# Projecting the values of two kinds of heads with tokens on partitions, ahead of the attention

## The chip, the cores and the metric

The kernel runs on one core of a Trainium2 chip. The metric is the device time of one execution in microseconds; the time of a version is the median of its runs. The core has five engines that work side by side, each through its own instructions in order: TensorE (PE, matmuls; its loads of the stationary operand are listed as PEld), VectorE (DVE), ScalarE (ACT), GpSimd (POOL) and SyncE (SP), from whose queue all transfers of this kernel are issued. Matmuls write to PSUM, from which ACT or DVE evict. Everything else lives in SBUF (128 partitions) or in DRAM.

## What is computed

One layer of a hybrid decoder on 1024 tokens of width 1024, in float32: half a SwiGLU, then a mixer of two groups of heads, then another half SwiGLU and a gated embedding. The change touches only the mixer:

```python
u = rmsnorm(h, mix_norm[i])
z = u @ w_in[i]
m_qk, m_v, m_o, m_if, f_q, f_k, f_v, f_f = jnp.split(z, split_idx, axis=-1)
m_qk = jax.nn.silu(causal_depthwise_conv(m_qk, conv_qk[i]))
...
h_m = mlstm_chunkwise(...)          # 4 heads, values m_v of width 128
...
h_f = forgetting_attention(...)     # 8 heads, values f_v of width 64
...
h = h + jnp.concatenate([y_m, y_f], axis=-1) @ w_out[i]
```

Both m_v and f_v are 512 columns of z. In the FoX attention a value block of 128 keys by 64 columns is multiplied from the right to the probabilities of 128 queries; in the mLSTM a block of 128 tokens by 128 columns goes into the state and into the output of a chunk. Both need the values with tokens on partitions.

## The kernel before

**Precision.** Matmuls run in float32r. Each operand is split into hi (a rounded copy, made by ACT) and lo (the rest, a subtraction on DVE, or on POOL where `aside` is set); `split_from` (line 100) does this. `mm3` (line 93) adds the three products hi·hi, hi·lo and lo·hi, so a product over k = 1024 for 512 columns takes 8 k tiles x 3 = 24 matmuls.

**The input of the mixer** is `xt`: the normalized tokens, transposed, so that a k tile has 128 channels on partitions and 512 tokens in its row, as (hi, lo), for each half of the tokens and each half of k.

**Projections.** `proj_stream` (line 625) takes jobs of 128 columns of w_in. Weights of a job are loaded in one transfer (`raw_cols`, line 57), split one job ahead, and used as the stationary operand; xt is the moving one. The result of a job and a half of the tokens is one PSUM bank with 128 columns of z on partitions and 512 tokens in a row. A sink takes it from there. For values a sink copies it to SBUF with ACT, PE transposes its four blocks of 128 x 128, and an eviction puts them where the attention reads them: for the mLSTM `v_sink` and `v_turn` (lines 867 to 879) into `v1`; for FoX `v_sink` and its `back` (lines 1073 to 1088) into `V[p]`, one tile for a pair of heads, which holds hi and lo side by side.

**Order of the mixer.** `mlstm` (line 831) first weaves the gates (DVE and ACT work, lines 716 to 828, with their tiles in the pool `gp`) with the projections of q and k, whose sink adds the convolution (DVE) and the Silu (ACT). Then the mLSTM values are projected, lines 894 to 899. Then the chunks run (`main`, line 901), with the output gate's projection as fill. `fox` (line 1026) projects values, queries and keys of the first pair of heads (line 1236) and then weaves `attention()` with `fill()`: the projections of the other three pairs, in the order values, queries, keys, and then `out_m`, the mLSTM part of the output projection (line 1259).

**weave** (line 605) emits two streams so that they advance together: each yields its time on PE as an estimate, and fill is emitted until it has `frac` times what the main stream has. A stream that can't go on yields None. In `jobs(p)` (line 1091) values of pair p may start when the values of the head that last used their buffer are done (`used`), queries and keys when the scores of the head that last used their tiles are done (`free`). A head is scores (line 1098: two or three matmuls for each 128 queries and 512 keys, a maximum on DVE, an exponential on ACT), transposes of the probabilities (line 1161), their split, and products with `V` (line 1141). Some work is put off by a number of steps with `later` (line 1174). `attention()` waits at the head of each pair until `done["proj"]` says that its keys are there.

The program's order is not kept to the letter: the compiler orders instructions of an engine by priority (their order in the program) among those that it takes to be ready, and it places tiles in pools, where a tile waits until the one that had its place before is done with.

Of the kernel before, what the change touches and what calls it, by code (L numbers as in the profile page):

```python
# [16 lines left out]
P = 128  # L17
# [7 lines left out]
# pairs of dff tiles, and the order of the seven block products of a Winograd form  # L25
# [4 lines left out]
class Net:  # L30
# [26 lines left out]
    def raw_cols(self, w, c0):  # L57
        """128 columns of a [1024, N] weight: row k * 128 + p at [p, k]."""
        r = self.rp.tile([P, KT, P], F32, tag="raw", name="raw")
        self.nc.sync.dma_start(out=r, in_=w[:, c0:c0 + P].rearrange("(k p) n -> p k n", p=P))  # L60
        return r
# [6 lines left out]
    def split(self, raw, pool=None, tag="w", aside=False):  # L68
        """raw = hi + lo, both in float32r."""
# [7 lines left out]
    def split2(self, raw, aside=False):  # L77
        """The two halves of k of a weight tile, each (hi, lo)."""
        return [self.split(raw[:, 4 * j:4 * j + 4, :], aside=aside) for j in range(2)]
# [13 lines left out]
    def mm3(self, out, ahi, alo, bhi, blo, first, last):  # L93
        """out (+)= a.T @ b with a = ahi + alo and b = bhi + blo."""
# [5 lines left out]
    def split_from(self, hi, lo, src, aside=False):  # L100
        """src (PSUM or SBUF) = hi + lo; aside: on GpSimd (SBUF only)."""
# [8 lines left out]
    def norm_rows(self, src, gain, dst):  # L110
        """dst = RMSNorm(src) * gain for 128 tokens; dst also takes the squares."""
# [7 lines left out]
    def xunit(self):  # L119
        """Four k tiles by 512 columns, (hi, lo)."""  # L120
        return tuple(self.xp.tile([P, 4, 512], F32R, tag=t, name=t) for t in ("xhi", "xlo"))

    def new_xt(self):
        """[half of the tokens][half of the k tiles] -> (hi, lo)"""
        return [[self.xunit() for _ in range(2)] for _ in range(2)]

    def normer(self, src, gain, dst):
        """RMSNorm of one token tile after another, transposed and split into dst(i) -> (hi, lo).
        Returns step(i), which takes token tile i and finishes the one before; step.rows(i) only takes it,
        step.next() only finishes the oldest."""  # L130
# [31 lines left out]
    def wino_put(self, B, name, rows, i):  # L162
        """512 columns of token tile i, transposed, into a right operand."""
# [10 lines left out]
    def wino_normer(self, src, gain, B, rows, bufs):  # L174
        """RMSNorm of one token tile after another into the right operands of the seven products
        (x transposed: rows k < 512 and k >= 512, columns t < 512 and t >= 512, Winograd's form).
        Three operands wait in DRAM for wino_rest. step(i) takes token tile i and finishes the one
        before, step.last() finishes the last."""
# [43 lines left out]
    def wino_rest(self, B, name):  # L222
        """One of the operands that wait in DRAM, through its place for lo."""
# [9 lines left out]
    def swiglu(self, B, w_gate, w_up, pools):  # L233
        """hidD = silu(x @ w_gate) * (x @ w_up), transposed, by pairs of dff tiles; the products of a
        pair (2 x 2 blocks: dff tile, half of k, half of the tokens) in Winograd's form with seven
        block products, each of three float32r products."""
# [3 lines left out]
        def pair(m, which, s):  # L240
            """Appends the seven products of the dff tiles m, m + 1."""
# [13 lines left out]
            # the first pair's tile a is loaded again for the sums  # L255
# [18 lines left out]
            def slot(r, c):  # L274
                """Where block (dff tile r, token half c) is put together."""
# [7 lines left out]
            def out(r, c, x, y, t):  # L283
                """Block (r, c) is x + y."""
# [8 lines left out]
            def hidden(r, c):  # L293
                """The left operands of the product with w_down: A11 = H00, A12 = H10, A21 = H01, A22 = H11
                (H: dff tile, half of the tokens), S1 = A21 + A22, S2 = S1 - A11, S3 = A11 - A21, S4 = A12 - S2."""
# [58 lines left out]
            # block (0, 0) = P1 + P2, (0, 1) = P1 + P6 + (P5 + P3), (1, 1) = P1 + P6 + P7 + P5,  # L354
            # (1, 0) = P1 + P6 + P7 + P4 (T4 is negated)
# [3 lines left out]
        for m in range(0, DFF // P, 2):  # L359
            s = {}  # L360
            g, u = pair(m, 0, s), pair(m, 1, s)
            # the first products don't need the second half of the tokens, those after them not T2, T3, T4
# [20 lines left out]
    def down(self, h, w_down, hook):  # L383
        """h += 0.5 * hid @ w_down in Winograd's form (2 x 2 blocks: half of the tokens, parity of the dff
        tile, half of the columns), one of the seven products after the other. Yields after the first loads
        and after the first operands; hook(j, q) runs after pair q of product j (the last one in two parts,
        4 and 8, of 256 tokens each)."""
# [20 lines left out]
        def fetch(j, q):  # L408
            """The left operands of two pairs."""
# [11 lines left out]
        def prep(n):  # L421
# [19 lines left out]
            # in place: T1 = B12 - B11, T3 = B22 - B12, T2 = B22 - T1, T4 = B21 - T2  # L441
# [18 lines left out]
        with tc.tile_pool(reuse_waits="tile", name="dn", bufs=1, side="right") as dn, \  # L460
# [11 lines left out]
            def evict(j, i):  # L472
                """Returns what can wait."""
# [18 lines left out]
            # C11 = P1 + P2, C12 = P1 + P6 + P5 + P3, C22 = P1 + P6 + P7 + P5, C21 = P1 + P6 + P7 + P4  # L492
            # (T4 is negated)
# [22 lines left out]
    def ffn(self, h, gain, w_gate, w_up, w_down, norms, hook, bufs, early=False, release=None):  # L516
        """h += 0.5 * SwiGLU(RMSNorm(h)); norms(step, prepare, products, pools, load_gain) runs the normalization
        over the token tiles, prepare() has the first weights split; early: products(n) may run there."""
# [39 lines left out]
    def ple_rows(self, p, w_proj, ps):  # L558
        """ppD = p @ w_proj; yields after every product of 128 tokens by 512 columns."""
# [45 lines left out]
def weave(main, fill, frac):  # L605
    """Emit main and fill so that they advance together: fill gets frac of main's TensorE time.
# [904 lines left out]
```

## Time and profile before

| | |
|---|---|
| runs shown, median (lowest to highest) | 2029.75 us (2027.75 to 2033.62), 3 runs |
| span of the profiled execution | 2033.1 us |
| mLSTM values, projections of lines 896 to 899 | from 756.4 to about 806 us |
| chunks of the mLSTM | 806 to 896 us |
| first FoX projections | 896 to 927 us |
| FoX attention with its fill | 931 to 1215 us |
| rest of out_m, then the output projection | from 1215 us |

The page gives no time of the profiled execution other than its span; the span lies between the median and the highest of the runs shown. In the views, a row of a timeline has start, duration, engine, line, operation, operands and, in brackets, the idle time of the engine before it with what ended it. A row of a table of stretches has the stretch and its length, then for each engine the busy time with the number of instructions, then the granted TensorE clock, the DMA engines' busy share and GB/s. A row of a group ends with busy time, mean ns of one, and the idle time before its instructions. Matmuls are pipelined: a row's duration overlaps that of its neighbours, so the distance of starts, not the duration, is what a matmul takes of PE.

### The profile page before, as it was taken

How to read it: one execution, taken by the hardware profiler on the slowest of the kernel's cores; microseconds unless marked ns; L12 is line 12 of the kernel's file. 1: busy time of each engine (PE TensorE's matmuls, PEld its weight loads, DVE VectorE, ACT ScalarE, POOL GpSimd, SP SyncE). 2: the span in 40 equal slices, each digit the busy share in tenths (PEclk: the TensorE clock that was granted, in tenths of full speed). 3: DMA queues.
4: the chain of work that ended last, by engine and by line, in shares of the span. 5: the costliest groups of instructions: out<-in, count | busy, mean ns of one | idle time of the engine just before them, and what ended most of it. 6: DMA issues, size and time to landing. Idle time of an engine off the chain costs nothing. (4 is left out here: it accounts for less than half of the span.)

```text
span 2033.1 us, 25588 instructions
## 1 busy us (share of the span) xinstructions
PE 1982.7 (98%) x9251; PEld 1618.8 (80%) x9251; DVE 1408.4 (69%) x2425; ACT 856.9 (42%) x1634; POOL 135.9 (7%) x148
## 2 busy tenths in 40 slices
PE   7999999999999999999999999999999999999998
PEld 6788888888888787788788777788888888888786
DVE  6966766777877683655565665877777777886766
ACT  6433333334445443435565642433333333444443
POOL 2000000000000110121110411100000000000011
PEclk9999999999999999999999999999999999999999
DMA  7623322338432331122112538533223237633422
GB/s 284 207 89 104 112 96 95 104 112 310 149 101 99 111 86 53 42 95 53 53 54 78 190 122 289 197 106 112 94 94 124 89 99 243 234 104 102 131 70 86
DMA packets 205359, 252.62 MB, mean 124 GB/s; under 512 B 12632, under 2 KB 138096, under 8 KB 204464
## 3 DMA queue, kind: packets, MB, share of 16 engines
q1 hardware_dynamic: 205232, 250.99, 37.8%
q8 instruction: 72, 1.18, 0.2%
q14 instruction: 55, 0.45, 0.1%
HBM read 172.18 MB, written 74.58 MB: 121 GB/s over the span
## 5 line engine op out<-in xcount | busy, mean ns | idle before, releaser
L96 PE MATMUL pp<-xhi,whi 128*128 128x512 f32 x704 | 275.6, 391 | 0.5 <-DVE s L272 0.5
L98 PE MATMUL pp<-xhi,wlo 128*128 128x512 f32 x704 | 274.1, 389 | 0.8 <-DVE wlo L103 0.8
L97 PE MATMUL pp<-xlo,whi 128*128 128x512 f32 x704 | 274.7, 390 | 0.0
L102 ACT CAST whi<-raw 128x512 fp32r<-128x512 f32 x180 | 111.3, 621 | 257.4 <-PE pp L97 177.2
L102 ACT CAST whi<-S 128x512 fp32r<-128x512 f32 x176 | 109.5, 622 | 240.8 <-PE pp L97 186.2
L96 PE MATMUL dn<-xhi,whi 128*128 128x512 f32 x528 | 205.7, 390 | 0.1
L97 PE MATMUL dn<-xlo,whi 128*128 128x512 f32 x528 | 205.5, 389 | 0.0
L98 PE MATMUL dn<-xhi,wlo 128*128 128x512 f32 x528 | 205.1, 389 | 0.0
L102 ACT CAST whi<-ar 128x512 fp32r<-128x512 f32 x132 | 82.3, 623 | 183.3 <-PE dn L97 174.8
L98 PEld LDWEIGHTS pp<-xhi,wlo 128*128 128x128 f32 x704 | 132.3, 188 | 29.2 <-DVE wlo L103 1.2
L96 PEld LDWEIGHTS pp<-xhi,whi 128*128 128x128 f32 x704 | 132.3, 188 | 29.1 <-DVE s L272 0.8
L97 PEld LDWEIGHTS pp<-xlo,whi 128*128 128x128 f32 x704 | 132.3, 188 | 27.7 <-DVE xlo L103 0.3
L103 DVE TENSOR_TENSOR wlo<-raw,whi 128x512 fp32r<-128x512 f32 x162 | 110.5, 686 | 59.7 <-ACT whi L102 46.7
L103 DVE TENSOR_TENSOR wlo<-S,whi 128x512 fp32r<-128x512 f32 x176 | 120.1, 682 | 25.8 <-ACT whi L102 25.7
L103 DVE TENSOR_TENSOR wlo<-ar,whi 128x512 fp32r<-128x512 f32 x132 | 90.7, 687 | 63.9 <-ACT whi L102 63.8
L96 PEld LDWEIGHTS dn<-xhi,whi 128*128 128x128 f32 x528 | 99.1, 188 | 21.0 <-DVE t L272 0.5
L98 PEld LDWEIGHTS dn<-xhi,wlo 128*128 128x128 f32 x528 | 99.1, 188 | 20.7
L97 PEld LDWEIGHTS dn<-xlo,whi 128*128 128x128 f32 x528 | 99.1, 188 | 20.6
L272 DVE TENSOR_TENSOR p<-pp,p 128x512 f32<-128x512 f32 x88 | 60.6, 689 | 74.9 <-PE pp L98 74.9
L107 POOL TENSOR_TENSOR r<-v,mhalf 128x1 f32<-128x1 f32 (+1 forms) x56 | 43.9, 784 | 909.6 <-DVE v L116 756.1
L96 PE MATMUL pj<-xhi,whi 128*128 128x512 f32 x248 | 102.6, 414 | 0.1
L97 PE MATMUL pj<-xlo,whi 128*128 128x512 f32 x248 | 97.5, 393 | 0.0
(350 smaller groups left out, 4515.0 us busy)
## 6 DMA issues: line engine op xcount, KB each, us to landing
ar<-hidD SPq DMA_DIRECT2D x60, 512.0 KB, 3.6
hidD<-t SPq DMA_DIRECT2D x110, 256.0 KB, 3.4
raw<-in_ffn_w_gate_dram SPq DMA_DIRECT2D x46, 512.0 KB, 3.9
raw<-in_ffn_w_up_dram SPq DMA_DIRECT2D x46, 512.0 KB, 3.7
raw<-in_w_in_dram SPq DMA_DIRECT2D x24, 512.0 KB, 3.9
hidD<-x SPq DMA_DIRECT2D x44, 256.0 KB, 3.1
ar<-hidD SPq DMA_DIRECT2D x32, 256.0 KB, 2.9
w<-in_ffn_w_down_dram SPq DMA_DIRECT2D x8, 1024.0 KB, 11.1
```

Source lines behind the costliest of these rows:

```text
L96: mm(out, ahi, bhi, start=first, stop=False)
L97: mm(out, ahi, blo, start=False, stop=False)
L98: mm(out, alo, bhi, start=False, stop=last)
L102: self.nc.scalar.copy(out=hi, in_=src)
L103: (self.nc.gpsimd if aside else self.nc.vector).tensor_tensor(out=lo, in0=src, in1=hi.bitcast(F32), op=ALU.subtract)
L107: self.nc.gpsimd.tensor_tensor(out=r, in0=v, in1=self.mhalf[:, :v.shape[-1]], op=ALU.pow)
L272: add = lambda d, x, y: nc.vector.tensor_tensor(out=d, in0=x, in1=y, op=ALU.add)
```

## The change

The values of both groups are projected in `mlstm`, one group after the other, before the chunks. The tokens are now the stationary operand (128 tokens of a k tile of xt), and 512 columns of weights, all of a group, the moving one. A result is one PSUM bank with 128 tokens on partitions and all 512 value columns in its row, so nothing is transposed.

Weights come as four loads of two k tiles with whole rows of 512 columns. Their split tiles have two pools: `va` for k tiles 0 to 3, filled while the last q and k projection runs, and `vb` for k tiles 4 to 7, in the space of the gates' pool once that is closed. The weights of the FoX values replace those of the mLSTM values k tile by k tile during the last token tile. The tiles `G1` and `qw` move into a pool `ml` in the space of `va` and `vb`.

The mLSTM values are evicted by one copy for each token tile. The FoX values are evicted as hi (ACT) and lo (DVE) in the layout of `V` and stored to a new DRAM tile `vD`, 512 KB for each token tile. In `fox`, `load_v(p)` brings back the 1 MB of a pair: pairs 0 and 1 after the first projections, pairs 2 and 3 when the values of the pair before last in the same buffer are done. `jobs(p)` has queries and keys alone, and the `frac` of the weave goes from 1.13 to 0.9. The rest of the diff takes out comments and docstrings.

```diff
+        self.vD = self.dp.tile([P, NT, 4, 4, 64], F32, tag="vD", name="vD")
...
-            G1 = mk.tile([P, 4, S], F32, tag="G1", name="G1")
-            qw = mk.tile([P, 2, S], F32, tag="qw", name="qw")
...
+                        if ct == 3:
+                            weights(C_MV, 0, 4)
...
-            def v_sink(hd):
-                def sink(half, acc):
-                    vt = mt.tile([P, 512], F32, tag="vt", name="vt")
-                    nc.scalar.copy(out=vt, in_=acc)
-                    turned.append((vt, half, hd))
-                return sink
-
-            def v_turn():
-                vt, half, hd = turned.pop(0)
-                pt = N.tr()
-                for j in range(4):
-                    nc.tensor.transpose(pt[:, j, :], vt[:, j * P:(j + 1) * P], N.ident)
-                nc.vector.tensor_copy(out=v1[:, 4 * half:4 * half + 4, hd, 0:128], in_=pt)
...
+            W, raws = {}, {}
+
+            def weights(c0, lo, hi):
+                for k in range(lo, hi):
+                    if k % 2 == 0:
+                        raws[0] = N.rp.tile([P, 2, 512], F32, tag="raw", name="raw")
+                        nc.sync.dma_start(out=raws[0], in_=self.w[k * P:(k + 2) * P, c0:c0 + 512].rearrange("(k p) n -> p k n", p=P))
+                    W[k] = [vp[k // 4].tile([P, 512], F32R, tag=f"{t}{k}", name=t) for t in ("vhi", "vlo")]
+                    N.split_from(W[k][0], W[k][1], raws[0][:, k % 2, :])
+
+            def token_values(c0, after, sink):
+
+                for i in range(NT):
+                    acc = bank()
+                    ts = slice((i % 4) * P, (i % 4) * P + P)
+                    for k in range(KT):
+                        xh, xl = xt[i // 4][k // 4]
+                        N.mm3(acc, xh[:, k % 4, ts], xl[:, k % 4, ts], W[k][0], W[k][1], k == 0, k == KT - 1)
+                        if i == NT - 1:
+                            after(k)
+                    sink(i, acc)
+
+            def mv_sink(i, acc):
+                nc.scalar.copy(out=v1[:, i, :, 0:128], in_=acc.rearrange("p (a b) -> p a b", a=4))
+
+            def fv_sink(i, acc):
+                t = N.rp.tile([P, 4, 4, 64], F32R, tag="raw", name="fv")
+                av = acc.rearrange("p (q a c) -> p q a c", q=4, a=2)
+                nc.scalar.copy(out=t[:, :, 0:4:3, :], in_=av)
+                nc.vector.tensor_tensor(out=t[:, :, 1:3, :], in0=av, in1=t[:, :, 0:4:3, :].bitcast(F32), op=ALU.subtract)
+                nc.sync.dma_start(out=N.vD[:, i], in_=t.bitcast(F32))
+
+            with ExitStack() as vs:
+                vpool = lambda name: vs.enter_context(self.tc.tile_pool(reuse_waits="tile", name=name, bufs=1))
+                vp = [vpool("va")]
+                with self.tc.tile_pool(reuse_waits="tile", name="gp", bufs=1) as gp:
+                    g = self.gates(xt, keep, gp, bank)
+                    next(g)
+                    weave(g, proj_stream(N, self.w, xt, [(C_MQK + ct * P, qk_sink(ct), None) for ct in range(4)], bank, self.begun[1]), 1.7)
+                vp.append(vpool("vb"))
+                weights(C_MV, 4, KT)
+                token_values(C_MV, lambda k: weights(C_FV, k, k + 1), mv_sink)
+                token_values(C_FV, lambda k: None, fv_sink)
+            ml = pool("ml", bufs=1)
+            G1 = ml.tile([P, 4, S], F32, tag="G1", name="G1")
+            qw = ml.tile([P, 2, S], F32, tag="qw", name="qw")
...
-            for n, _ in enumerate(proj_stream(N, self.w, xt, [(C_MV + hd * P, v_sink(hd), None) for hd in range(4)], bank)):
-                if n % KT == 3 and turned:
-                    v_turn()
-            v_turn()
...
-            def v_sink(p):
...
+            def load_v(p):
+                V[p] = xq.tile([P, NT, 4, 64], F32R, tag="V", name="V")
+                nc.sync.dma_start(out=V[p].bitcast(F32), in_=N.vD[:, :, p])
...
-                used = lambda: 2 * p - 2 <= done["values"]
-                return [(C_FV + p * P, v_sink(p), used), (C_FQ + p * P, q_sink(p), free), (C_FK + p * P, k_sink(p), free)]
+                return [(C_FQ + p * P, q_sink(p), free), (C_FK + p * P, k_sink(p), free)]
...
                         if qb == 3:
-                            done["values"] = hd + 1
+                            if hd % 2 and hd < 5:
+                                load_v((hd + 3) // 2)
...
             run_all(proj_stream(N, self.w, xt, jobs(0), bank))
+            for p in range(2):
+                load_v(p)
...
-            weave(attention(), fill(), 1.13)
+            weave(attention(), fill(), 0.9)
```

## What was predicted

> **What bounds the kernel now.** I read the page first (totals, then the 40 slices), then the busy time by stage, then the stage that the change touches instruction by instruction.
>
> ```profile
> span 2033.1 us, 25588 instructions
> PE 1982.7 (98%) x9251; PEld 1618.8 (80%) x9251; DVE 1408.4 (69%) x2425; ACT 856.9 (42%) x1634; POOL 135.9 (7%) x148
> ```
>
> TensorE has work for 98% of the span. The table of stretches (length, then busy us of PE, PEld, DVE, ACT, POOL, then granted clock and DMA share) shows where that holds:
>
> ```profile
> 756.00:770.00 14.00, 14.00 (x65) 11.60 (x64) 11.18 (x15) 6.14 (x5) 0.00 (x0) 1.00 0.20 47
> 770.00:782.00 12.00, 10.92 (x52) 8.75 (x52) 3.94 (x6) 4.29 (x8) 0.00 (x0) 1.00 0.17 45
> 782.00:806.00 24.00, 24.00 (x113) 19.30 (x112) 5.39 (x9) 5.09 (x9) 0.00 (x0) 1.00 0.16 44
> 896.00:927.00 31.00, 31.00 (x142) 25.66 (x141) 10.98 (x16) 10.84 (x19) 5.72 (x5) 1.00 0.42 130
> 931.00:1215.00 284.00, 267.12 (x1518) 219.86 (x1517) 177.51 (x387) 161.96 (x416) 50.74 (x34) 0.99 0.29 89
> ```
>
> The mLSTM values (756 to 806) and the first FoX projections (896 to 927) are filled by PE to the brim, but for 1.08 us at 771. The FoX attention (931 to 1215) is different: 16.9 us of its 284 are idle, and its busy time is modelled. There PE executes two kinds of work in one order: projection matmuls ("fill", tile acc) and attention instructions. I price both.
>
> ```profile
> 755.95 0.39 PE L98 MATMUL pj<-xhi,wlo 128*128 128x512 f32 x1
> 764.11 0.39 PE L98 MATMUL pj<-xhi,wlo 128*128 128x512 f32 x1
> 764.34 0.60 PE L878 MATMUL tr<-ident,vt 128*128 128x128 f32 x4
> 764.70 0.48 PE L96 MATMUL pj<-xhi,whi 128*128 128x512 f32 x1
> 765.01 0.40 PE L97 MATMUL pj<-xlo,whi 128*128 128x512 f32 x1
> ```
>
> Between the first two rows lie 36 steps without a gap: 8.16 / 36 = 0.227 us for a 512-column matmul (the 0.39 of a row overlaps its neighbours). With four transposes between them, two matmuls start 0.59 us apart (764.11 to 764.70) and the next follows after 0.31, so the four cost 0.36 + 0.08 = 0.44 us.
>
> **The change part by part.** *Matmuls.* Each group of values keeps its 192 matmuls of 512 columns: before 4 column tiles x 2 halves of tokens x 8 k x 3, after 8 token tiles x 8 k x 3. Operands change sides, sizes don't: I cost the swap at nothing. The FoX group moves ahead of the mLSTM body: 192 x 0.227 = 43.6 us appear there, 48 x 0.227 = 10.9 leave the stretch 896 to 927, 144 x 0.227 = 32.7 leave the attention.
>
> *Transposes.* 64 go, in 16 groups of four: 8 among the mLSTM values, where PE is full, so 8 x 0.44 = **-3.5 us**; 8 in the attention, another **-3.5 us** if PE sets the pace there, 0 if it doesn't; I take -3.5, because 267 busy of 284 is nearer to that end.
>
> By the Trainium skill, "TensorE: Matmul & The Clock Gate", Part 4, a transpose on TensorE was seen at some 275 ns, which would make 64 of them worth 17.6 us (an estimate from that page); the durations in this trace agree, but the starts above show 0.11 us each on the path, and the measurement decides.
>
> *Evictions.* What goes:
>
> ```profile
> L879 DVE COPY v<-tr 128x512 f32<-128x512 f32 x8 | 5.5, 688 | 5.0 <-PE tr L878 5.0
> L1088 DVE TENSOR_TENSOR V<-tr,V 128x512 fp32r<-128x512 f32 x8 | 5.5, 686 | 1.3 <-ACT V L1087 1.1
> L1078 ACT COPY fvt<-acc 128x512 f32<-128x512 f32 x6 | 3.5, 591 | 1.3 <-PE acc L98 1.3
> 771.51 0.66 PE L878 MATMUL tr<-ident,vt 128*128 128x128 f32 x4 [1.08 <-ACT vt L870]
> 766.84 3.63 ACT L864 ACTIVATE qk<-qk 128x4096 f32<-128x4096 f32 x1 [3.09 <-DVE qk L861]
> ```
>
> After, each token tile has one ACT copy, for FoX also one DVE subtraction, beside 5.4 us of matmuls (24 x 0.227): hidden while DVE and ACT are a quarter busy (row 782 to 806); uncovered it would be 0.7 us a tile. The stall of 1.08 us (a copy queued behind the 3.63 us of Silu) changes form: with two accumulator buffers the third token tile still waits for a copy behind Silu. I take 0, bounds -1.1 and +1.5.
>
> *Weights.* Before, the first product needs one column tile (two splits); after, one token tile needs all eight k tiles in its first 5.4 us. k 0 to 3 are split early. k 4 to 7 lie in space that the gate tiles leave, and DVE is full then:
>
> ```profile
> 758.43 1.22 DVE L810 TENSOR_TENSOR T<-G,T 8x1024 fp32r<-8x1024 f32 x1
> 760.18 0.68 DVE L813 TENSOR_SCALAR lf<-T 8x1024 fp32r<-8x1024 f32 x1
> 740.71 0.62 ACT L102 CAST whi<-raw 128x512 fp32r<-128x512 f32 x1 [1.86 <-PE pj L97]
> 760.89 0.26 SPq L815 DMA_DIRECT2D crow<-lf  x1
> 760.89 1.29 DVE L103 TENSOR_TENSOR wlo<-raw,whi 128x512 fp32r<-128x512 f32 x2
> 762.88 3.92 DVE L861 SCALAR_TENSOR_TENSOR qk<-zin,pcol,qk 128x1024 f32<-128x1024 f32 x3
> ```
>
> PE wants k 4 at 756.4 + 12 x 0.227 = 759.1. The gate tile G is read until 759.65, lf leaves by DMA from 760.89 (some 2 us more, as "yD<-yhi" below). Two more splits than before by then put DVE 1.3 us later, so k 4 is there at about 762, k 6 and 7 at 765, or at 768 when they fall behind the convolution (762.88 + 3.92 + 1.3). Nothing pulled ahead, PE stands 2.9 us before k 4 (759.1 to 762), 4.6 before k 6 (763.4 to 768) and 0.6 before k 7: 8 us. If it takes the second token tile's k 0 to 3, then its k 4 and 5, in between (2.7 us each), it reaches 761.8 and 764.6, and only 0.2 + 0.4 = 0.6 us are left. I take **+3**, nearer to the lower end, because this trace does run ready work ahead of stalled work (the first mLSTM value weights, of which the row at 740.71 is one, are split before copies that the program has earlier). Behind the waiting cast on ACT stand Silu and the copies; behind them the third token tile, counted above. The FoX weights replace k by k during the last token tile: freed 0.7 us apart, one ACT cast (0.62) and one DVE subtraction (0.69) each, needed 5.4 us later: nothing.
>
> *DMA.* Eight weight loads of 512 KB stay eight of 512 KB. New: eight stores of 512 KB and four loads of 1 MB.
>
> ```profile
> yD<-yhi SPq DMA_DIRECT2D x4, 256.0 KB, 2.1
> w<-in_ffn_w_down_dram SPq DMA_DIRECT2D x8, 1024.0 KB, 11.1
> 928.11 1.79 SPq L1067 DMA_DIRECT2D k<-k  x2
> 931.13 0.28 PE L1111 MATMUL sc<-k,q 128*128 128x128 f32 x1
> 908.58 0.22 SPq L1063 DMA_DIRECT2D k<-crow  x1
> 917.19 1.81 SPq L1053 DMA_DIRECT2D q<-q  x2
> ```
>
> The stores run beside matmuls at a DMA share of 0.16. The loads of V[0] and V[1] are behind the k copies on SP, and those release the first scores 3.0 us after issue; if they were put ahead, two loads of some 11 us would stand in front. First use is some 40 attention instructions later (about 6 us). Cost 0 to +5 (11 us less those 6); I take 0, because SP issues nothing from 909 to 917 and the loads fit there. The loads for pairs 2 and 3 wait on SP for the last product of V's old tile, with weight loads and q and k copies behind them, but two heads (70 us) ahead of use: 0.
>
> *The attention without its fill.* Following weave() with the costs that it yields: before, V1 runs beside head 0 and V2, V3 need only earlier values; after, Q1, Q2, Q3 need scores of heads 0, 2, 4. Attention instructions of PE in runs without fill: before 60 and 76 and 33 (169 in all), after 54, 101 and 48 + 101 on end (304). The trace has such runs; first all PE, then tile acc alone:
>
> ```profile
> 955.00:960.00 5.00, 5.00 (x33) 4.34 (x33) 2.42 (x5) 2.57 (x7) 0.00 (x0) 1.00 0.00 0
> 1070.00:1075.00 5.00, 4.61 (x33) 3.96 (x32) 4.55 (x11) 3.15 (x12) 0.00 (x0) 1.00 0.01 3
> 955.00:960.00 5.00, 3.22 (x12) 2.05 (x12) 0.00 (x0) 0.00 (x0) 1.00 0.00 0
> 1070.00:1075.00 5.00, 0.00 (x0) 0.00 (x0) 0.00 (x0) 0.00 (x0) 1.00 0.01 3
> 931.00:1215.00 284.00, 156.00 (x558) 99.09 (x557) 24.00 (x35) 17.59 (x30) 0.99 0.29 89
> ```
>
> Without fill: 33 instructions in 5 us, 0.152 each, DVE at 91%: DVE is the bound. Well filled: (5 - 12 x 0.227) / 21 = 0.108. Over the whole attention: (284 - 558 x 0.227) / 960 = 0.164, or 0.146 without the 16.9 us idle. So 135 more unfilled instructions cost 135 x (0.152 - 0.108) = 6 us at most and nothing at least; I take **+3**, the middle.
>
> **Sum**: -3.5 - 3.5 + 3 + 3 = -1 us on an execution of 2033.1 us span. The runs without profile have the median 2029.75, 3.35 less; the same difference on that gives **2028.7 us**. With every cost at its least: -7.0 - 1.1 + 0.6 = -7.5 (2022). With every cost at its most and no gain in the attention: -3.5 + 1.5 + 8 + 5 + 6 = +17 (2047).
>
> **The rivals.** 0.3% (6 us) is about what a measurement of this kernel can tell from no change.
>
> *A: faster.* Ready fill is pulled into the bare stretches, the second half of the weights is in time, and some of the waits for yn go:
>
> ```profile
> 927.00:931.00 4.00, 4.00 (x19) 3.21 (x18) 1.38 (x2) 2.92 (x4) 1.30 (x1) 1.00 0.45 96
> PE tr L1211 <- DVE yn L1204: 3.7, 2, 2.1
> PE tr L1161 <- DVE yn L1204: 3.6, 3, 1.8
> L103 POOL TENSOR_TENSOR wlo<-raw,whi 128x512 fp32r<-128x512 f32 x18 | 23.2, 1288 | 142.2 <-ACT whi L102 122.9 <-PE acc L98 19.3
> ```
>
> For it: 19 fill matmuls did run ahead of the first scores, while these waited for k. yn waits for a reciprocal root on POOL, and a third of the 18 splits there go. Against: in 1070 to 1075 no fill was pulled in. Time: -7.5, and up to the 7.3 us of those waits: -7.5 to -14.8, the middle 2019.
>
> *B: slower, by the weights.* The stall at k 4 to 7 takes its 8 us, the copy behind Silu 1.5, and a long idle lowers the clock as here:
>
> ```profile
> 990.00:995.00 5.00, 2.90 (x13) 2.03 (x12) 1.57 (x4) 0.84 (x2) 1.64 (x1) 0.85 0.00 0
> 995.00:1000.00 5.00, 5.00 (x30) 4.42 (x29) 3.32 (x6) 3.39 (x7) 1.28 (x1) 0.81 0.58 170
> ```
>
> An idle of 2.1 us is followed by some 3.4 us at half clock (0.15 x 5 + 0.19 x 5 = 1.7 us lost). Then -7 + 3 + 8 + 1.5 + 1.7 = +7, 2037. From a stall of 4 us on, this alone eats the gain (-7 + 3 + 4 = 0).
>
> *C: slower, by bare attention.* The 304 bare instructions run below full clock: at 0.81 they cost 304 x 0.152 x 0.23 = 10.6 us more; -1 + 10.6 gives 2039. Against it: the row 1070 to 1075 has 1.00.
> The Trainium skill speaks for C (same page, Part 4): transposes don't keep the clock up as other matmuls do; a third of the bare instructions are transposes. The trace has only 10 us of such a run, and its clock held.
>
> **How the numbers follow.** Forecast (within 6 us of 2029.75) 0.42; A 0.33; B 0.13; C, or the V loads in front of the k copies, 0.12. Faster by over 0.3%: 0.33. Within: 0.42. Slower: 0.25. The range reaches to A's middle and to C: 2016 to 2042.
>
> **What would show it.** Right: no transposes in the value stages; 24 matmuls per 5.4 us there; PE idle near 759 to 766 of some 3 us; attention plus its tail 30 to 34 us shorter than 284 + 11; stretches of 10 to 23 us without tile acc, DVE near 90%, 0.15 us an instruction. Wrong: such stretches at 0.11 (A) or 0.18 (C); an idle of 8 us before k 4 (B); PE waiting for V or k from DMA at the first scores; a clock under 1.00 for more than 5 us.

## The result and the profile after

The changed kernel takes 2042.68 us (median of 4 runs, 2041.89 to 2045.9), the kernel before 2029.30 (4 runs beside it): a ratio of 1.0063, 95% interval 1.005 to 1.0076. It is slower, by about 13 us. Forecast were 2028.7 and a range of 2016 to 2042, which the time misses by 0.7 us; "within 0.3%" was held likeliest, and it is outside.

The page of the changed kernel begins:

```profile
span 2040.1 us, 25466 instructions
PE 1981.0 (97%) x9187; PEld 1616.8 (79%) x9187; DVE 1403.9 (69%) x2423; ACT 851.6 (42%) x1626; POOL 127.3 (6%) x142
```

Against the page of before there are 64 PE instructions fewer (the transposes), PE is busy for 1.7 us less, and the span is 7.0 us longer. The two profiles are two single executions. A run's time is some 1.8 us longer than its span (2041.89 and 2040.1 for the profiled run of the changed kernel), so by this estimate the profiled execution of before took some 2034.9 us, 5.6 above the median of its runs, and that of after lies 0.8 below its median. Only 7.0 of the 13.4 us can therefore be followed from row to row, and a stage that differs by two or three us between two profiles says little. The rest is read from medians of experiments.

The table of stretches of the changed kernel, with the columns explained above:

```profile
756.00:760.00 4.00, 4.00 (x19) 3.29 (x18) 3.77 (x6) 1.55 (x2) 0.00 (x0) 1.00 0.52 138
760.00:765.00 5.00, 1.59 (x7) 0.79 (x5) 4.86 (x7) 0.00 (x0) 0.00 (x0) 1.00 0.14 22
765.00:770.00 5.00, 0.12 (x1) 0.12 (x1) 1.18 (x1) 3.79 (x2) 0.00 (x0) 0.55 0.00 0
770.00:775.00 5.00, 5.00 (x12) 3.85 (x13) 2.50 (x4) 3.78 (x6) 0.00 (x0) 0.50 0.41 117
775.00:780.00 5.00, 5.00 (x22) 4.07 (x21) 0.00 (x0) 1.18 (x2) 0.00 (x0) 0.93 0.27 93
780.00:856.00 76.00, 76.00 (x336) 62.16 (x336) 10.35 (x15) 12.82 (x22) 0.00 (x0) 1.00 0.15 56
855.00:860.00 5.00, 4.16 (x21) 2.25 (x19) 3.08 (x6) 3.15 (x6) 0.00 (x0) 1.00 0.58 170
860.00:865.00 5.00, 5.00 (x16) 3.74 (x16) 3.71 (x7) 2.32 (x7) 0.00 (x0) 0.66 1.14 345
960.00:1235.00 275.00, 258.13 (x1451) 212.30 (x1449) 176.51 (x391) 156.31 (x405) 49.25 (x35) 0.98 0.38 119
```

From 780 on the values run nearly as the sum wanted them: PE is full, and 341 matmuls start 0.229 us apart between 777.20 and 855.25 (0.227 in the prediction, which makes 0.9 us for 384). Two places are new: PE all but idle from 761 to 770, then 12 matmuls in 5 us at half clock (770 to 775); and 16 instructions in 5 us at a clock of 0.66 where the chunks begin (860 to 865).

The stages, from the starts of the last or first matmul of a kind in the timelines of the two kernels. Two of these borders need a look, the end of the values before (the output gate's projection starts at 804.96) and the last key matmul after, ahead of which fill of the attention (tile acc) already runs:

```profile
804.22 0.39 PE L98 MATMUL pj<-xhi,wlo 128*128 128x512 f32 x1
804.96 0.50 PE L96 MATMUL pj<-xhi,whi 128*128 128x512 f32 x1
...
963.63 0.39 PE L98 MATMUL acc<-xhi,whi 128*128 128x512 f32 x1
971.37 0.39 PE L100 MATMUL pj<-xhi,wlo 128*128 128x512 f32 x1
```

| | before | after | difference |
|---|---|---|---|
| values ahead of the chunks | 756.2 to 804.2: 48.0 us | 755.5 to 855.3: 99.8 us | +51.8 (moved in: 43.6; transposes: -3.5) |
| from there to the last key matmul of the first pair, less the first projections (32.7; 21.8) | 89.7 | 94.3 | +4.6 (fill that runs ahead: 2.5) |
| from that key matmul to the end of out_m | 926.6 to 1225.9: 299.3 | 971.4 to 1234.0: 262.6 | -36.7 (moved out: 32.7; transposes: -3.5) |

The attention gave 36.7 us, about what the two parts in brackets promise together (36.2). But 11 of its fill matmuls (11 x 0.227 = 2.5 us) had run by 971.4, and before none had by 926.6, so 34.2 is nearer the truth; what is behind that comes with the transposes below. The loss is in the two stages ahead of it: 11.7 us more than expected in the values (51.8 less 40.1; the first place below has 8.3 + 2.5 of it), and in the chunks 2.1 behind the fill, on which the prediction has no term.

**The first place.** PE, then DVE and ACT, in the timeline of the changed kernel:

```profile
760.76 0.40 PE L100 MATMUL pj<-vhi,xlo 128*128 128x512 f32 x1
761.09 0.50 PE L932 MATMUL wd<-RW,sel 36*128 36x512 f32 x1
769.88 0.79 PE L960 MATMUL st<-qk 64*128 64x128 f32 x2 [8.30 <-ACT qk L866]
...
772.05 0.63 PE L100 MATMUL pj<-vhi,xlo 128*128 128x512 f32 x1
772.48 0.63 PE L98 MATMUL pj<-vhi,xhi 128*128 128x512 f32 x1
...
775.81 0.39 PE L100 MATMUL pj<-vhi,xlo 128*128 128x512 f32 x1
...
762.25 3.93 DVE L863 SCALAR_TENSOR_TENSOR qk<-zin,pcol,qk 128x1024 f32<-128x1024 f32 x3
770.37 2.50 DVE L105 TENSOR_TENSOR vlo<-raw,vhi 128x512 fp32r<-128x512 f32 x4 [4.19 <-ACT vhi L104]
...
766.22 3.62 ACT L866 ACTIVATE qk<-qk 128x4096 f32<-128x4096 f32 x1 [8.65 <-DVE qk L863]
769.74 2.16 ACT L104 CAST vhi<-raw 128x512 fp32r<-128x512 f32 x4
```

PE finished k 0 to 3 of two token tiles at 761.1 and took one matmul of the chunks (wd). The bracket of the next row names the Silu, but look at what follows it: the four casts of k 4 to 7 stand *behind* Silu in ACT's order, all four at 769.74. ACT idles 8.65 us ahead of Silu, waiting for the convolution, while the casts queue behind. So PE has nothing to do for 8.3 us, whichever of the two the bracket names. Then matmuls start 0.43 us apart (772.05 to 772.48) instead of 0.227 until about 775.6: 12 x 0.2 = some 2.5 us more. By the Trainium skill, "TensorE: Matmul & The Clock Gate", Part 1 ("What's actually happening"), the clock falls to half after at least one idle window of some 3.4 us and returns after at least one busy window as long, and these windows run on freely and don't start with the kernel. The fall and the return agree: by the slices the clock fell at about 765.5, some 3.9 us after the last matmul (an estimate from 1.00 and 0.55), and the return took 5.7 us (769.9 to 775.6), between one window and two.

**The second place.** Transfers as SP issued them, in the timeline of the changed kernel (the duration of a row spans its issues):

```profile
818.56 33.28 SPq L908 DMA_DIRECT2D vD<-fv  x7
851.95 0.38 SPq L62 DMA_DIRECT2D raw<-in_w_in_dram  x1
857.02 0.32 SPq L908 DMA_DIRECT2D vD<-fv  x1
857.43 7.05 SPq L62 DMA_DIRECT2D raw<-in_w_in_dram  x5
...
860.09 0.50 PE L98 MATMUL pj<-xhi,whi 128*128 128x512 f32 x1
```

The eight FoX value tiles are written into `raw`, the four buffers through which all weights are staged, and each holds one until its store is done. The output gate's first weights are requested at 851.95, when the values are 3.6 us from their end, and its first matmul starts at 860.09. A buffer still in use is only a part of that. The request needs the buffer of the fifth store if buffers are taken in turn, and that store was issued at 840.53, with the DMA engines idle from 843 to 845. But on SP the request stands behind the seventh store, and SP waits some 5 us for the data of each (DVE's fv); only one of the weight loads waits for a store by name, in the list of SP's waits:

```profile
SPq L62 <- DMA vD<-fv: 1.3, 1, 1.3
```

So what the shared buffers bring about is for the most part an order, loads behind stores. The gate's projection was meant as fill for the chunks; without it the chunks run bare, and at a lowered clock. In the timeline of before, the gate's matmuls already stand at 805, among the first chunk instructions.

### The profile page after: what moved, and what is told of

The parts are those of the page before. It is cut to its first block, busy times and chain, and to the rows that moved or that the text cites. A ratio compares the mean times of both kernels' runs of the same rounds, so it can differ in the third digit from the quotient of the medians.

```text
span 2040.1 us, 25466 instructions
## 1 busy us (share of the span) xinstructions
PE 1981.0 (97%) x9187; PEld 1616.8 (79%) x9187; DVE 1403.9 (69%) x2423; ACT 851.6 (42%) x1626; POOL 127.3 (6%) x142
## 5 line engine op out<-in xcount | busy, mean ns | idle before, releaser
L104 ACT CAST whi<-raw 128x512 fp32r<-128x512 f32 x164 | 101.1, 622 | 234.0 <-PE pp L99 175.5
L99 PEld LDWEIGHTS pp<-xlo,whi 128*128 128x128 f32 x704 | 132.2, 188 | 27.7 <-DVE xlo L105 0.2
L105 DVE TENSOR_TENSOR wlo<-raw,whi 128x512 fp32r<-128x512 f32 x152 | 103.6, 686 | 34.7 <-ACT whi L104 32.4
L289 ACT ACTIVATE s<-s 128x512 f32<-128x512 f32 x88 | 55.7, 633 | 80.5 <-DVE s L274 80.3
L98 PE MATMUL pj<-xhi,whi 128*128 128x512 f32 x168 | 71.7, 427 | 0.1
```

Of the source, the lines that this page charges most:

```text
L98: mm(out, ahi, bhi, start=first, stop=False)
L99: mm(out, ahi, blo, start=False, stop=False)
L104: self.nc.scalar.copy(out=hi, in_=src)
L105: (self.nc.gpsimd if aside else self.nc.vector).tensor_tensor(out=lo, in0=src, in1=hi.bitcast(F32), op=ALU.subtract)
L289: nc.scalar.activation(out=t, in_=t, func=AF.Silu)
```

## The experiments

Theory: two causes. (1) Weights of k 4 to 7 are late, behind the convolution and Silu, and PE has no other work. (2) FoX value stores, in the buffers of the gate's weights, keep these weights back. Rivals: the attention with less fill beside it pays more; what the change saves (transposes) is worth less than counted. The runs of before beside these experiments have medians of 2029.4 to 2030.7, so a difference between two groups of runs can carry about 1 us of that.

**More work ahead of k 4 (wide).** In the mLSTM values five token tiles take k 0 to 3 first, in five PSUM banks that the chunks use later; then each takes k 4 to 7.

```diff
-                for i in range(NT):
-                    acc = bank()
+                wide = 5 if c0 == C_MV else 0
+                for i in range(wide):
+                    accs[i] = bank() if i < 2 else mps.tile([P, 512], F32, tag="ST", name="pj", bufs=2) if i < 4 else \
+                        mps.tile([P, 512], F32, tag="D", name="pj")
+                    part(i, range(4))
+                for i in range(NT):
...
+                    part(i, range(4, KT))
+                    sink(i, accs[i])
```

> The changed kernel, but five token tiles of the mLSTM values take k 0 to 3 first, in five PSUM banks (before: two). Theory W: the changed kernel loses some 11.5 us at 761 to 776, because k 4 to 7 are split only after the Silu and the scores of the first chunk, pulled ahead, wait for it as well (9.0 us of waiting, and 12 matmuls at 0.43 instead of 0.23 us after it). Then 13.6 us of matmuls fill the gap up to 769, some 1.5 us of waiting are left, and the time is about 2032.5. Rival: the whole stage is late by its vector work (gates, convolution, eight splits), and the wait only moves to the next token tile: 2038 or more.

2032.81 us (10 runs), ratio to before 1.0013 [1.0001, 1.0025]; 9.9 us less than the changed kernel. In its list of PE's waits the 8.3 us are gone:

```profile
PE pj L98 <- ACT vhi L104: 1.0, 1, 1.0
```

The values take 89.5 us (754.2 to 843.6) where 384 x 0.229 = 87.9 is bare work. The weights were not earlier; PE had 5 x 12 x 0.227 = 13.6 us to do until they came. What is left is the second place, now at 845 to 860. In wide's table of stretches:

```profile
845.00:850.00 5.00, 3.45 (x11) 1.49 (x11) 3.03 (x6) 3.66 (x6) 0.00 (x0) 0.93 0.80 235
850.00:855.00 5.00, 5.00 (x14) 3.62 (x14) 3.24 (x7) 2.76 (x7) 0.00 (x0) 0.50 1.05 310
855.00:860.00 5.00, 5.00 (x16) 4.15 (x15) 1.28 (x6) 0.38 (x1) 0.00 (x0) 0.55 0.28 85
```

**Buffers of their own for the FoX values, with that (wide_fv) and alone (fv_own).**

```diff
-                t = N.rp.tile([P, 4, 4, 64], F32R, tag="raw", name="fv")
+                t = vf.tile([P, 4, 4, 64], F32R, tag="fv", name="fv")
...
+                vf = vs.enter_context(self.tc.tile_pool(reuse_waits="tile", name="vf", bufs=2))
```

> As wide, and the FoX value tiles on their way to DRAM have two buffers of their own instead of the four that weight loads use. Theory M: in the changed kernel the output gate's weights wait for these stores (issued at 852, first matmul at 860), so the chunks start without fill and then run at a lowered clock; the stage is 6.8 us longer than before. Then this gives another -6: about 2026.5, a little under the kernel before. Rival: the chunks start slowly by their own chain (exponentials, first products) wherever they start: no gain over wide, 2032.5.

> The changed kernel, only the FoX value tiles have two buffers of their own. Theory M: the wait at 761 to 776 stays, the chunks start with fill at once and keep their clock, the stretch of the chunks is 91 us as in wide_fv instead of 94.4: 2042.7 - 3.3 = 2039, at best 2042.7 - 7.5 = 2035 (the gain that it gave over wide). Rival (the two losses are one, a wait hidden behind the other): no change, 2042.

wide_fv: 2025.29 us (12 runs), ratio 0.998 [0.997, 0.9989]. It is faster than both kernels, 17.4 us less than the changed one. fv_own: 2036.72 (4 runs), 1.0041 [1.0025, 1.0056]. So by the medians the buffers are worth 6.0 us alone (2042.7 to 2036.7) and 7.5 beside wide; the late weights 9.9 alone and 11.4 beside fv_own. fv_own stands between the two times of its theory, and its rival (2042) fell. By the chunk stage of the profiles (94.3 in the changed kernel, 98.6 in wide, 91.6 in fv_own, 91.1 in wide_fv) the buffers come to 2.8 alone and 7.5 beside wide: the size alone is uncertain, the two together, 17.4 us, are not. (The 6.8 us in the expectation counts the stage of before from 806.7, when some matmuls of the gate had already run; from 804.2 it is 4.6, fill included.) SP and PE in the timeline of wide_fv:

```profile
797.25 8.85 SPq L62 DMA_DIRECT2D raw<-in_w_in_dram  x6
806.83 38.77 SPq L919 DMA_DIRECT2D vD<-fv  x8
...
843.84 0.50 PE L944 MATMUL wd<-RW,sel 36*128 36x512 f32 x1
844.27 0.50 PE L98 MATMUL pj<-xhi,whi 128*128 128x512 f32 x1
```

Weight loads now stand ahead of the stores, and the gate's projection starts right with the chunks. How much of this is the free buffer and how much the order on SP wasn't separated. The granted clock is 1.00 in every five-microsecond slice from 840 to 875 (0.50 to 0.55 in wide from 850 to 860).

**Silu behind the casts (silu_behind).** Silu gets a bias of zero that is made from the last cast of k 7, so it must follow it; its result is the same.

```diff
-                            nc.scalar.activation(out=qk, in_=qk, func=AF.Silu)
...
+                bz = N.sp.tile([P, 1], F32, tag="bz", name="bz", bufs=1)
+                nc.scalar.mul(out=bz, in_=W[7][0][:, 0:1].bitcast(F32), mul=0.0)
+                nc.scalar.activation(out=qk, in_=qk, func=AF.Silu, bias=bz)
```

> The changed kernel, with the Silu made to follow the last hi cast of k 7 (its bias is that cast's first column times 0). If the Silu alone keeps k 4 to 7 back, they are there at about 764 and the wait shrinks from 9.0 to some 2 us: about 2033. If the place that the gates leave (their last transfer is issued at 761.5) and the convolution ahead of the lo parts on VectorE hold them as well, k 4 comes at about 767 and the wait is 6 to 7 us; 2039 or so.

A single run: 2035.85 us, between the two. From 760 to 770 PE stands for 2.84 us, against 8.29 in the changed kernel, and by 780 it has started 71 of the value matmuls, against 55. In silu_behind's timeline and table of stretches:

```profile
763.46 2.17 ACT L104 CAST vhi<-raw 128x512 fp32r<-128x512 f32 x4
764.29 1.22 PE L98 MATMUL pj<-vhi,xhi 128*128 128x512 f32 x2
...
760.00:765.00 5.00, 3.54 (x11) 1.77 (x9) 4.86 (x7) 2.63 (x5) 0.00 (x0) 0.87 0.14 22
765.00:770.00 5.00, 3.62 (x9) 2.49 (x8) 3.64 (x6) 4.35 (x6) 0.00 (x0) 0.50 0.26 66
```

The casts run 6.3 us earlier (763.46, in the changed kernel 769.74). ACT's order is therefore the larger part of the wait but not all of it: the casts still start some 1.5 us behind the prediction's 762, DVE has 4.86 of 5 us with the gates and the convolution, and the weights' lo parts are made on DVE (PE waits 1.4 us for the first). The clock fell here too (0.50). How the rest divides between the gates' space and DVE's queue wasn't tried.

**FoX alone (old_mv, old_mv_fv).** The mLSTM values are projected and transposed as before, the FoX values as in the change; in old_mv_fv these have their own buffers too.

```diff
-                weights(C_MV, 4, KT)
-                token_values(C_MV, lambda k: weights(C_FV, k, k + 1), mv_sink)
+                for n, _ in enumerate(proj_stream(N, self.w, xt, [(C_MV + hd * P, v_sink(hd), None) for hd in range(4)], bank)):
+                    if n % KT == 3 and turned:
+                        v_turn()
+                    if n == 2 * KT * 3:
+                        weights(C_FV, 0, KT)
+                v_turn()
```

> The changed kernel with the mLSTM values projected and transposed as before; only the FoX values are new. Theory W: no wait at 761 to 770, 32 transposes back (+3.5): 2042.7 - 11.5 + 3.5 = 2034.5, and the stretch of the chunks still some 6 us longer than before. Rival (the loss sits in the attention without its fill): 2040 or more, since the attention is unchanged.

> old_mv with the FoX value tiles in two buffers of their own. Theory M: its stretch of the chunks, 98.7 us by the milestones of its trace (from the last FoX value product to the end of the first keys, less 21.8), shrinks to some 91: 2038.9 - 7.6 = 2031.3. Against wide_fv (2025.3) that leaves 32 transposes (3.5) and its wait of 2.2 us behind the Silu. Rival: the chunks are late for another reason: 2037 or more.

old_mv: 2038.92 us (4 runs), 1.0044 [1.0027, 1.0061], 4.4 us over the theory's number and near the rival's: its trace has no late weights any more but has the second place in full, the stores at 811.52 and the gate's weights only at 844.90, with a granted clock of 0.50 from 855 to 860. With own buffers, 2031.38 (10 runs), 1.0008 [0.9999, 1.0017]: 7.5 us less, the same price as between wide and wide_fv. Without the second cause the FoX half of the change thus gains nothing that shows; the mLSTM half brings the 6.1 us from there to wide_fv; 2.2 of them are a wait for a copy behind Silu that old_mv_fv still has.

**What the transposes are worth (before_no_tr).** The kernel before, with its 64 transposes of values left out: the evictions copy the untransposed tile.

```diff
-                pt = N.tr()
-                for j in range(4):
-                    nc.tensor.transpose(pt[:, j, :], vt[:, j * P:(j + 1) * P], N.ident)
+                pt = vt.rearrange("p (a b) -> p a b", a=4)
```

> The kernel before without its 64 transposes of values: the evictions read the untransposed copy instead, so the values are in the wrong place. It sizes the gain that the prediction gave to the transposes alone: 16 groups of 0.44 us, 7.0 in all (2023.7); 3.5 if those in the attention cost nothing (2027.2).

2021.22 us (5 runs), 0.9963 [0.9951, 0.9976]: 8.2 us less than its runs of before, 0.13 for each transpose. How they divide between the values and the attention isn't shown: from the last key matmul to the end of out_m this kernel takes 292.3 us and before 299.3, but these two profiled executions are 13.7 us apart in span, not 8.2. The price of less fill beside the attention can be read from it: 292.3 less the 32.7 moved out is 259.6, and the changed kernel, which has no value transposes either, takes 262.6, so 3.0 us more, or 5.5 with the 2.5 us of fill that it had done by then. These are single profiles, both near their medians; in the other kernels with frac 0.9 that stretch has 261.2 to 262.8.

**The attention without its fill (bare, fv_f113, fv_f06).** wide_fv with another `frac` in the weave: 3.0 spends nearly all fill at once, 1.13 is the value of the kernel before, 0.6 saves fill for later.

```diff
-            weave(attention(), fill(), 0.9)
+            weave(attention(), fill(), 3.0)
```

> wide_fv with the weave's frac 3.0 instead of 0.9: all fill is emitted as early as it may, so that nearly all 928 attention instructions stand in runs without fill (by my count of the order 928 instead of 304). Theory: an attention instruction costs some 0.16 us with or without fill beside it and fill costs its own 0.227, so nothing changes: 2025, within 3. Rival (the prediction's term: 0.152 bare against 0.108 filled): 624 x 0.044 = 27 us more, 2052; with my middle value half of it, 2039.

> The kernel wide_fv (five token tiles at once in the mLSTM values, FoX value tiles in their own pool) with frac 1.13 in the weave of the attention, as in the kernel before, in place of 0.9. By the order of the program it has 408 attention instructions of PE without fill around them instead of 304, the longest such stretch 220 instead of 149, and still a little fill behind them all. Theory 1 (a bare instruction costs what a filled one costs as long as the stretches are short and fill is left for the end): 2025.3, within 2 us of wide_fv. Rival (each bare instruction costs what the run 'bare' gives on average, 35.6 / 624 = 0.057 us): 104 x 0.057 = 6 us more, 2031.

> wide_fv with frac 0.6 in place of 0.9: less fill runs beside the first heads. By the order of the program 448 attention instructions are without fill (the keys of a pair are then still unfinished when the attention comes to it, so fill is drawn alone there, and the rest of it is emitted behind the attention), the longest stretch 183; much of out_m is left for the tail. Theory 1: within 2 us of 2025.3, or a little below, since the tail (the last head's back part and the load of yfh) has more fill beside it. Rival: 144 x 0.057 = 8 us more, 2033.

Measured: 3.0 gives 2060.92 us (4 runs, 1.0161 [1.0148, 1.0175]), 1.13 gives 2051.85 (4 runs, 1.0109 [1.0094, 1.0123]), 0.6 gives 2039.51 (6 runs, 1.0051 [1.0035, 1.0068]). All three are far above wide_fv: the theory that bare stretches cost nothing fell three times, and so did the rival's flat 0.057 us for each instruction (6 us expected for 1.13, some 27 measured). The number of bare instructions alone is not what counts. With 1.13, PE's timeline ends the attention like this:

```profile
1223.67 0.44 PE L1216 MATMUL tr<-ident,O 128*128 128x128 f32 x2 [1.58 <-DVE O L1171]
1228.22 1.12 PE L1234 MATMUL tr<-ident,yn 128*128 128x128 f32 x4 [4.11 <-DVE yn L1227]
1237.75 0.80 PE L98 MATMUL acc<-wf,yfh 128*128 128x512 f32 x1 [8.42 <-DMA yfh<-yD]
1238.34 0.63 PE L99 MATMUL acc<-wf,yfh 128*128 128x512 f32 x1
```

After the last product with V (1221.5) come its eviction, the norm (yn), its transposes and a trip through DRAM (yfh); the output projection can only start 16.2 us later, and if out_m is used up by then, PE stands still and then starts at half clock (matmuls 0.43 to 0.6 apart). The same three times in the timelines of all:

| kernel | frac | last product with V | out_m ends | output projection starts |
|---|---|---|---|---|
| before | 1.13 | 1206.5 | 1225.9 | 1226.1 |
| after | 0.9 | 1215.5 | 1234.0 | 1234.3 |
| wide_fv | 0.9 | 1199.1 | 1217.6 | 1217.9 |
| fv_f113 | 1.13 | 1221.5 | 1216.4 | 1237.8 |
| fv_f06 | 0.6 | 1195.3 | 1233.0 | 1233.2 |
| bare | 3.0 | 1235.0 | 1157.6 | 1251.1 |

At 0.9 the rest of out_m covers that tail with 18.5 us, just over the 16 it needs. At 1.13 and 3.0 nothing covers it. At 0.6 it is covered by 37.7, and the 20 us too many were missing beside the heads: PE idles 27.7 us from 950 to 1220, in wide_fv 18.3 (150 + 120 less its busy time in the tables of stretches). That is 9.4 of the 14.2 us by which 0.6 is slower; the clock from 1100 to 1220 is also lower (0.94, in wide_fv 0.97). The change of `frac` belongs to the change: 144 of the fill's matmuls are gone from the attention. In bare, the last 75 us had no fill at all; rows of its table of stretches:

```profile
1160.00:1170.00 10.00, 8.60 (x58) 7.21 (x58) 8.23 (x23) 7.34 (x22) 0.00 (x0) 1.00 0.42 141
1170.00:1180.00 10.00, 8.00 (x49) 7.07 (x48) 6.70 (x18) 7.85 (x20) 4.74 (x2) 0.85 0.16 52
1200.00:1210.00 10.00, 7.77 (x35) 6.64 (x35) 7.19 (x15) 6.74 (x18) 4.27 (x3) 0.66 0.18 52
1210.00:1220.00 10.00, 7.86 (x55) 6.65 (x56) 9.44 (x25) 7.56 (x23) 0.00 (x0) 1.00 0.15 56
```

Taken as one stretch, the 75 us from 1160 have 358 recorded instructions, 0.209 us each. The changed kernel, counted in the same way over 25 us with little fill (1075 to 1100, shown below), has 0.165, so this makes 358 x 0.044 = 16 us more. With the tail's 16 that accounts for 32 of the 35.6 us by which bare is slower than wide_fv; the rest isn't followed.

## Why the prediction was wrong

| term | predicted | found | by |
|---|---|---|---|
| tokens as the stationary operand | 0 | +0.9 | 0.229 us a matmul in after |
| 64 transposes | -7.0 | -8.2 | before_no_tr |
| weights of k 4 to 7, the copy behind Silu, the clock | +3 (0.6 to 8; 1.5 and 1.7 apart) | +9.9 to +11.4 | wide, wide_fv against fv_own |
| stores of the FoX values | 0 | +6.0 to +7.5 (2.8 to 7.5 by the stage) | fv_own, wide_fv, old_mv_fv |
| loads of V | 0 | no wait of PE for them in the list of waits | after |
| attention with less fill | +3 (0 to 6) | +3.0 to +5.5 | after against before_no_tr |

With the two waits taken together, 0.9 - 8.2 + 17.4 + 3.0 = +13.1, or +15.6 with 5.5 for the attention; measured were +13.4. In the same way wide_fv, which has neither wait, should stand at -4.3, or -1.8, and stands at -4.1 by its ratio (0.998 of 2030.7) and at -5.4 by the medians. So the sum closes with the lower figure for the attention, and some 2 us stay open with the upper one. In wide_fv the chunks with the first projections take 91.1 us, 1.4 more than before, and here too 2.5 of it is fill that runs ahead: no loss is left in that stage.

**The weights.** The place, the mechanism and the idle beforehand were as the prediction had them: PE took k 0 to 3 of the second token tile, and stood from 761 on. The step that failed is the next: "If it takes the second token tile's k 0 to 3, then its k 4 and 5, in between (2.7 us each), it reaches 761.8 and 764.6, and only 0.2 + 0.4 = 0.6 us are left." It took k 4 to be there at about 762. It came after 769.74, since all four casts stood behind Silu on ACT. The prediction had written the order the other way round: "Behind the waiting cast on ACT stand Silu and the copies". Even its upper bound of 768 (behind the convolution) was short by Silu's 3.62 us. Rival B was this mechanism, priced at 2037: with 8.3 us of wait and 2.5 of clock it was nearly right in size, and alone would have given 2036.7 (fv_own), but it had a chance of 0.13. In silu_behind, without that order, PE takes k 4 at 764.29, 2.3 us after 762. The reason for choosing the lower half, that this trace runs ready work ahead of stalled work, holds only where there is ready work: the third token tile had no bank.

**The stores.** "The stores run beside matmuls at a DMA share of 0.16" is the step that failed by kind. The DMA engines had indeed room (0.15 from 780 to 856), but the cost wasn't one of bandwidth: stores and weight loads shared four buffers, and the gate's loads came to stand behind the stores. The diff shows it in one word, `tag="raw"`; the prediction asked of the loads of V where SP would issue them, but not of the gate's weights, and not which tile had to be free for them. Priced at 0, this cost 6.0 to 7.5 us. Both causes together, 17.4 us, are the difference between the changed kernel and wide_fv.

**The attention.** The +3 for bare instructions was the middle of 0 to 6, not worked out further; 3.0 to 5.5 were found, so it was about right in size. The duration behind it was right too. The changed kernel has 17 projection matmuls in the 25 us from 1075 to 1100; its table of stretches:

```profile
1075.00:1080.00 5.00, 4.88 (x35) 4.14 (x34) 4.58 (x11) 3.69 (x11) 0.00 (x0) 1.00 0.51 120
1080.00:1085.00 5.00, 4.66 (x34) 3.78 (x32) 3.82 (x12) 4.35 (x14) 0.00 (x0) 1.00 0.01 3
1085.00:1090.00 5.00, 3.76 (x28) 3.10 (x27) 3.85 (x9) 1.73 (x4) 1.64 (x1) 1.00 0.00 0
1090.00:1095.00 5.00, 4.70 (x28) 3.29 (x26) 4.44 (x11) 3.90 (x14) 0.00 (x0) 1.00 0.14 41
1095.00:1100.00 5.00, 4.78 (x29) 4.05 (x30) 4.21 (x13) 3.46 (x11) 0.00 (x0) 1.00 0.83 277
```

The other 137 of the 154 instructions take (25 - 17 x 0.227) / 137 = 0.154 us each (0.152 was predicted), at full clock. Both figures are a little low, because a slice also counts the instructions that cross its edges: the 25 us taken as one stretch have 145, and 0.165 for each of the other 128. What the prediction didn't ask is what the new `frac` does at the end of the attention; 0.9 happens to fit, and had it stayed at 1.13, the loss would have been some 27 us more, if it costs there what it cost in wide_fv. Rival C (a lowered clock in bare stretches) isn't borne out: the nearly bare 25 us above ran at 1.00. The clock did fall elsewhere in the changed kernel's attention, to 0.77 from 1145 to 1150 and 0.50 from 1180 to 1185, where PE had waited 2.4 and 2.9 us in the slices from 1145 and from 1175; before has two such places as well (990 to 1000 and 1135 to 1145). In bare, over 75 us, the clock fell to 0.66 in places. The Trainium skill's sentence on transposes and the clock ("TensorE: Matmul & The Clock Gate", Part 4) could be at work in that long stretch alone, but there PE also waits, and no run here separates the two. Rival A (faster) fell by the same two waits; without them wide_fv gives 2025.3, between the forecast and A's 2019.

**The range** was to reach "to A's middle and to C", which are 2019 and 2039; its ends of 2016 and 2042 lie 3 us beyond them, and no reason is given. That it missed by only 0.7 us is luck: B and C were each priced alone, and a term put at nothing (the stores) was in no case.

## What to carry to other kernels

Where a change makes the first tile of a stage need all of an operand instead of a part, write down, engine by engine, what stands in front of the last piece of it, and give PE enough independent accumulators to bridge that time: here five banks instead of two were worth some 10 us. When a tile is stored from a pool that also stages loads, the loads can come to stand behind the stores: give the stores their own buffers, even two. When fill moves out of a woven stretch, choose its rate anew so that what is left at the end covers the last item's tail (here 16 us), and no more.

## What the runs showed of the hardware that was not expected

A wait costs more than itself. After 8.3 us without a matmul the clock stayed at half for 5.7 us under full load, and matmuls of 512 columns started 0.43 us apart instead of 0.227: 2.5 us on top of 8.3. A stage that isn't idle can lose the clock as well: in wide PE has work for all of 850 to 860, yet the granted clock is 0.50 and 0.55, after 1.55 us of idle and small chunk matmuls in the slice before, the longest single gap being 0.69 us.
